# First feed-forward with four plain columns in place of six, and the third group's sums moved behind the last gate product

## The chip, the cores and the metric

The kernel runs on one core of a Trainium2 chip. The metric is device time in microseconds (us) of one execution; the time of a kernel is the median of several. Engines are named as in the profile: PE is TensorE's matrix product, PEld its weight loads, DVE is VectorE, ACT is ScalarE, POOL is GpSimd, SP issues most transfers.

## What is computed

The reference is a trunk of two layers on 512 positions of 1024 channels, in float32. Each layer has a half-step feed-forward, a mixer (a bidirectional state-space scan in layer 0, neighbourhood attention in layer 1), a second half-step feed-forward and a gated embedding:

```python
def swiglu(x, w_gu, w_down):
    g, u = jnp.split(x @ w_gu, 2, axis=-1)
    return (jax.nn.silu(g) * u) @ w_down

for i in range(DEPTH):
    h = h + 0.5 * swiglu(rmsnorm(h, ffn1_norm[i]), ffn1_w_gu[i], ffn1_w_down[i])
    h = h + mixer(rmsnorm(h, mix_norm[i]))
    h = h + 0.5 * swiglu(rmsnorm(h, ffn2_norm[i]), ffn2_w_gu[i], ffn2_w_down[i])
    gate = jax.nn.sigmoid(rmsnorm(h, ple_norm[i]) @ ple_w_gate[i])
    h = h + gate * rmsnorm(p[i] @ ple_w_proj[i], ple_post_norm[i])
```

So there are four feed-forwards. The inner width is 2816, which is 22 columns of 128.

## The kernel before

Everything is kept transposed: 128 channels on the partitions, the 512 positions along the free dimension, so `h` is eight tiles of 128 x 512. Full precision comes from splitting each operand in a high and a low part (ACT casts the high part, L231, L327; DVE subtracts it, L233, L328) and three matmuls for each product: high by high (L298), high by low (L301) and low by high (L302). A **weight unit** is 128 x 1024 numbers; three split units may be ready at a time (`bufs=3` of `wh` and `wl`), and `prep_next` splits the next one in the order that `plan` lists. `unit` takes one and refills.

A feed-forward (`ffn`) goes through its 22 columns in five chunks, `FIRST` for the first one of the kernel, `OTHERS` for the other three. `ffn_order` lists the steps:

- **Plain columns**: those of the first chunk, six in the first feed-forward, four in the others. `gate_up` forms the gate product and the other product of a column, two units of 24 matmuls each. They use `h` times the gain, without the norm; the reciprocal norm `R` is ready only after the first matmuls (`spread`, L379, then L381 to L388), and `activate` (L474 to L478) multiplies the products by it, applies the activation and splits the result into `mids[f]`.
- **Pairs of output tiles**: the down products of the first chunk for output tiles 0 to 3, two side by side (`side_by_side`). They need `mids` of all columns of the chunk.
- **Blocks**: the other columns two at a time. A pair of columns, both gate and other product, is a product of 2 x 2 blocks, done with seven block products in place of eight (`block`, matmuls at L539). Each block has one weight unit that is a sum or difference of the pair's quadrants (formed on DVE at L254, L257, L259, L276) and one input that is a sum or difference of halves of the normed `h`. These inputs, `xs`, are made once for each feed-forward by `sums(kk)` for four groups kk = 0 to 3 (L498 to L525), each with DVE work of about 5 us and casts on ACT; they need `R`. Blocks run in the order `TURN`: 0, 3, 1, 4, 5, 2, 6; blocks 0, 1, 2 and 6 take matmuls of 512 and 256 positions, the others three of 256. Every block reads all four groups.
- **Down products**, spread among the next chunk's blocks (L614, L629 add them to `h`).

In the first feed-forward columns 0 and 1 are computed while the inputs arrive (`first`), without `R`; column 2 is the first that ends with `R`.

Where `sums` is called before the change: in all feed-forwards group 0 stands behind the first `R` (L460, in `gate_up`). Each later plain column has one group in front of it (L604 and L605), and if one is left after the last plain column, it follows that column's activation (L469). In the first feed-forward this gives groups 0, 1, 2, 3 at columns 2, 3, 4, 5. In the others it gives groups 0, 1, 2 at columns 1, 2, 3 and group 3 behind column 3's activation.

The program order is not the engines' order. A planner (the tile framework's scheduler) walks over the program with costs of its own for each instruction and gives each engine's queue the ready instruction that comes first in the program, so a later instruction fills a gap in which an earlier one is not ready. The order is fixed when the kernel is built; on the chip each engine takes its instructions in that order. `tc.issue_after` adds an edge that keeps some of them behind another.

`plan` also sets when the first pair's four weight quadrants are fetched and summed: in the first feed-forward behind unit 6 (column 3), in the others behind unit 3.

Of the kernel before, what the change touches and what calls it, by code (L numbers as in the profile page):

```python
# [19 lines left out]
FF = 2816  # L20
NF = FF // P

FIRST = ((0, 6), (6, 10), (10, 14), (14, 18), (18, 22))
OTHERS = ((0, 4), (4, 8), (8, 12), (12, 16), (16, 22))
HT = T // 2
EPS = 1e-6
# [26 lines left out]
def ffn_order(chunks):  # L53

    for f in range(chunks[0][1]):
        yield "plain", f
    yield "pair", 0, 0
    yield "pair", 0, 2  # L60
    for c in range(1, len(chunks)):
        a, b = chunks[c]
        blocks = [(p, i) for p in range(a // 2, b // 2) for i in TURN]
        begun = d = 4 if c == 1 else 0
        for n, (p, i) in enumerate(blocks):
            yield "block", p, i
            while d < KD and (d - begun + 1) * len(blocks) <= (KD - begun) * (n + 1):
                yield "down", c - 1, d
                d += 1
    yield "between",  # L70
    for d in range(KD):
        yield "down", len(chunks) - 1, d
# [3 lines left out]
def trunk(ctx, tc, A, out):  # L76
# [76 lines left out]
    def plan():  # L153
# [3 lines left out]
        for i in range(stop):  # L157
            l, w = divmod(i, 4)
            if w in (0, 2):
                gu, gw, dn = [A[f"w_{x}{2 * l + w // 2}"] for x in ("gu", "gw", "dn")]  # L160
                chunks = FIRST if i == 0 else OTHERS
                plain = chunks[0][1]
# [115 lines left out]
    def unit(last=False):  # L278

        while (not last or not ready) and len(ready) < 3 and prep_next():  # L280
            pass
        return ready.pop(0)
# [10 lines left out]
    def gemm(pt, w, pairs, first=True, last=True, off=0, cols=slice(0, T), behind=False):  # L293
        hi, lo = w
        n = len(pairs)
        for k, xp in enumerate(pairs):
            sl = slice((off + k) * P, (off + k + 1) * P)
            m = te.matmul(out=pt, lhsT=hi[:, sl], rhs=part(xp, 0, cols), start=first and k == 0, stop=False)  # L298
            if behind and k == 0:
                tc.keep_in_program_order(m)  # L300
            te.matmul(out=pt, lhsT=hi[:, sl], rhs=part(xp, 1, cols), start=False, stop=False)  # L301
            gemm.last = te.matmul(out=pt, lhsT=lo[:, sl], rhs=part(xp, 0, cols), start=False,  # L302
                                  stop=last and k == n - 1)

    def side_by_side(pts, pairs, mid=None, at=4, then=None):

        ws = [unit() for _ in pts]
        k = len(pairs) - 1
        for pt, w in zip(pts, ws):
            c = min(at, k) if mid and pt is pts[-1] else k  # L310
            gemm(pt, w, pairs[:c], last=False)
            if mid and pt is pts[-1] and at <= k:
                mid()
            if then and c < k:
                gemm(pt, w, pairs[c:c + 1], first=False, last=False, off=c)
                then()
                c += 1
            if c < k:
                gemm(pt, w, pairs[c:k], first=False, last=False, off=c)
        for pt, w in zip(pts, ws):  # L320
            gemm(pt, w, pairs[k:], first=False, off=k)
        if mid and at > k:
            mid()
# [102 lines left out]
    def ffn(norm, nxt, between=None, first=None, at=4):  # L426
        R = [None]
# [4 lines left out]
        def mid():  # L432
            norm.begin()
            ahead(norm)

        def gate_up(f):
            pg = mm_bank()
            if not (first and R[0] is None and f == 2):
                pu = mm_bank()
            if first and f < 2:  # L440
                held.append((f, pg, pu))
                if f == 1:
                    first([p for x in held for p in x[1:]], norm.pairs)
                    mid()
                return
            if f == 0 and not first:
                side_by_side((pg, pu), norm.pairs, mid, at, lambda: norm.spread(AF.Silu))
                held.append((f, pg, pu))
                return
            if R[0] is None:  # L450

                w, c = unit(), 1
                gemm(pg, w, norm.pairs[:c], last=False)
                if first or at > len(norm.pairs) - 1:
                    norm.spread(AF.Silu)
                R[0] = norm.end()
                gemm(pg, w, norm.pairs[c:], first=False, off=c)
                while held:
                    activate(*held.pop(0))
                sums(left.pop(0))  # L460
                if first:
                    pu = px_bank()
            else:
                gemm(pg, unit(), norm.pairs)
            gemm(pu, unit(), norm.pairs)
            held.append((f, pg, pu))
            while held:
                activate(*held.pop(0))
            if left and f == chunks[0][1] - 1:  # L469
                sums(left.pop(0))  # L470

        def activate(f, pg, pu):
            gm = t2()
            v.tensor_mul(out=gm, in0=pg, in1=R[0])  # L474
            s.activation(out=gm, in_=gm, func=AF.Silu)
            um = t2()
            v.tensor_mul(out=um, in0=pu, in1=R[0])
            v.tensor_mul(out=um, in0=um, in1=gm)  # L478
            m = md(F32R)
            split(m, um, None)  # L480
            mids[f] = m
# [118 lines left out]
        made, left, owed = None, [0, 1, 2, 3], []  # L600
        chunks = FIRST if first else OTHERS
        for what, *a in ffn_order(chunks):
            if what == "plain":
                if left and R[0] is not None:  # L604
                    sums(left.pop(0))  # L605
                gate_up(a[0])
            elif what == "block":

                if between and a in ([chunks[-1][0] // 2, 0], [NF // 2 - 1, 4]):
                    next(between)  # L610
                block(*a)
                for d, pt in owed:
                    with tc.issue_after(block.last.ins):
                        v.scalar_tensor_tensor(out=h[d], in0=pt, scalar=0.5, in1=h[d], op0=ALU.mult, op1=ALU.add)  # L614
                owed = []
            elif what == "between":
                made = between and next(between)
            else:
                c, d = a
                last = c == len(chunks) - 1  # L620
                mine = [mids[f] for f in range(*chunks[c])]
                if what == "pair":
                    pts = [(mm_bank if d else px_bank)() for _ in range(2)]
                    side_by_side(pts, mine)
                    owed += [(d, pts[0]), (d + 1, pts[1])]
                    continue
                pt = mm_bank() if last else px_bank()
                gemm(pt, unit(last and d == KD - 1), mine)
                v.scalar_tensor_tensor(out=h[d], in0=pt, scalar=0.5, in1=h[d], op0=ALU.mult, op1=ALU.add)  # L629
                if last:  # L630
                    nxt(d)
                    if 1 < d < 5 and made is not None:
                        made[d - 1]()
# [905 lines left out]
    def first(pts, pairs):  # L1539
        done_ = [0] * 4  # L1540
        here, cut_ = 0, [0] * 4
        for o in order:
            if isinstance(o, int):
                here = o + 1
            else:
                cut_[o[0]] += 1
            for u in range(4):
                while done_[u] < min(here, 4 * cut_[u]):
                    k = done_[u]
                    gemm(pts[u], begun[u][2:], pairs[k:k + 1], first=k == 0, last=k == KD - 1, off=k)  # L1550
                    done_[u] += 1
        prep_next()

        with tc.issue_after(splits[-1].ins):
            for k in range(KD):
                n.count(k, True)
        while len(ready) < 3:
            prep_next()
# [17 lines left out]
def prepare(inp):  # L1576
    import numpy as np

    def units(w):
        k, n = w.shape[0] // P, w.shape[1] // P  # L1580
        return w.reshape(k, P, n, P).transpose(2, 1, 0, 3).reshape(n, P, k * P)
# [6 lines left out]
    for i in (1, 2):  # L1588
        gu = f[f"ffn{i}_w_gu"]
        for l in range(DEPTH):  # L1590
            k = 2 * l + i - 1
            plain = (OTHERS if k else FIRST)[0][1]
            g_ = units(gu[l]).reshape(2, NF, P, 1024).transpose(1, 0, 2, 3)
# [82 lines left out]
```

## Time and profile before

| what | value |
|---|---|
| median of 3 runs | 2274.69 us (2274.47 to 2274.8) |
| the profiled execution | 2274.88 us |
| its span, first to last instruction | 2273.0 us |
| granted TensorE clock | 0.999 |
| matmuls at L539 (blocks), four feed-forwards | 35 pairs, 4760 matmuls |

A page of the profile has busy time by engine, the chain of work that ended last, and groups of instructions. The timeline lists one engine's instructions: start in us, duration, engine, line, operation, tiles written and read, sizes, count; a bracket behind it gives idle time of the engine before it and what ended that. The chain of waits lists what the end of the execution hung on: start, length, engine and line. A row of the windows gives busy time of each engine in a stretch. Durations of matmuls are modelled, so their starts are what counts: a stream of 128 x 512 matmuls has durations of 0.39 us and starts 0.23 us apart. DVE's durations overlap by some 0.08 us with the next one's.

### The profile page before, as it was taken

To read this page: it belongs to the slowest core of one execution; us is meant where nothing else is said; L and a number is where in the kernel's file an instruction comes from. 1 tells how busy PE (TensorE), PEld (TensorE's weight loads), DVE (VectorE), ACT (ScalarE), POOL (GpSimd) and SP (SyncE) were. 2 spreads that over 40 slices of the span, in tenths; PEclk is the share of its full clock that TensorE was granted. 3 is DMA by queue.
4 is the path that set the end of the run, shared out by engine and by line. 5 is a ranking of instruction groups with operands and counts; after the bars stand their busy time and mean duration, and the time that the engine had idled before them with its cause. 6 is when DMAs were issued, how large, how long until landed. Compare 5 with 4: busy or idle time off the path is not lost.

```text
span 2273.0 us, 33245 instructions
## 1 busy us (share of the span) xinstructions
PE 2265.7 (100%) x12458; PEld 1948.5 (86%) x12458; DVE 1823.0 (80%) x2711; ACT 1284.3 (57%) x2335; POOL 327.9 (14%) x261
## 2 busy tenths in 40 slices
PE   9999999999999999999999999999999999999999
PEld 7888888888888888888888888888888888988887
DVE  8788878988888958988885898888668758888866
ACT  6444445777677765544457555444557655544563
POOL 0000001345555651000003100000110010000020
PEclk9999999999999999999999999999999999999999
DMA  5323324444444643322323332332557732333232
GB/s 198 114 77 107 107 78 140 162 154 140 146 141 143 208 146 120 116 98 85 102 89 115 108 102 88 98 107 78 173 176 228 227 117 92 103 107 107 79 102 75
DMA packets 105089, 281.56 MB, mean 124 GB/s; under 512 B 13008, under 2 KB 13904, under 8 KB 104928
## 3 DMA queue, kind: packets, MB, share of 16 engines
q1 hardware_dynamic: 104640, 279.30, 37.8%
q8 instruction: 98, 1.61, 0.3%
q14 instruction: 63, 0.52, 0.1%
q10 hardware_dynamic: 288, 0.14, 0.0%
HBM read 259.70 MB, written 13.40 MB: 120 GB/s over the span
## 4 chain that ended last, share of the span: by engine, by line
PE 96%; DVE 3%; ACT 1%; issue 0%; DMA 0%; POOL 0%; SPq 0%; DVEq 0%; POOLq 0%
PE ps L539 31%; PE ps L298 19%; PE ps L302 19%; PE ps L301 19%; PE ps L1023 1%; PE ps L982 1%; PE ps L1377 1%; PE ps L1003 1%; PE ps L1431 1%; PE ps L938 1%; PE ps L927 1%; PE ps L1420 1%; DVE wl L233 0%; DVE md L328 0%; PE ps L1411 0%
## 5 line engine op out<-in xcount | busy, mean ns | idle before, releaser
L298 PE MATMUL ps<-md,wh 128*128 128x512 f32 (+1 forms) x2032 | 796.0, 392 | 0.9 <-ACT md L327 0.9
L302 PE MATMUL ps<-md,wl 128*128 128x512 f32 (+1 forms) x2032 | 790.5, 389 | 0.2 <-DVE wl L233 0.2
L301 PE MATMUL ps<-md,wh 128*128 128x512 f32 (+1 forms) x2032 | 790.1, 389 | 0.0
L231 ACT CAST wh<-wr 128x1024 fp32r<-128x1024 f32 (+2 forms) x395 | 351.7, 892 | 417.4 <-PE ps L301 200.3
L233 DVE TENSOR_TENSOR wl<-wr,wh 128x1024 fp32r<-128x1024 f32 (+2 forms) x395 | 417.6, 1058 | 97.4 <-ACT wh L231 91.6
L302 PEld LDWEIGHTS ps<-md,wl 128*128 128x128 f32 x2032 | 381.5, 188 | 82.3 <-DVE wl L233 1.5
L298 PEld LDWEIGHTS ps<-md,wh 128*128 128x128 f32 x2032 | 381.6, 188 | 77.8 <-ACT md L327 1.4
L301 PEld LDWEIGHTS ps<-md,wh 128*128 128x128 f32 x2032 | 382.0, 188 | 74.0 <-DVE md L598 0.5
L539 PE MATMUL ps<-md,wh 128*128 128x256 f32 (+1 forms) x1610 | 367.2, 308 | 0.0
L539 PE MATMUL ps<-sc,wh 128*128 128x512 f32 (+1 forms) x1190 | 362.3, 357 | 0.0
L364 POOL TENSOR_TENSOR sq<-sq,sq 128x512 f32<-128x512 f32 x71 | 100.9, 1422 | 1612.1 <-ACT sq L360 1261.7
L233 DVE TENSOR_TENSOR wl<-md,wh 128x1024 fp32r<-128x1024 f32 x175 | 214.0, 1223 | 113.6 <-ACT wh L231 112.8
L231 ACT CAST wh<-md 128x1024 fp32r<-128x1024 f32 x175 | 183.8, 1051 | 200.9 <-PE ps L539 129.0
L539 PEld LDWEIGHTS ps<-md,wh 128*128 128x128 f32 x1610 | 263.7, 190 | 20.3
L539 PE MATMUL ps<-md,wl 128*128 128x256 f32 x980 | 276.4, 282 | 0.0
L539 PE MATMUL ps<-sc,wl 128*128 128x256 f32 x980 | 275.7, 281 | 0.0
L539 PEld LDWEIGHTS ps<-sc,wh 128*128 128x128 f32 x1190 | 210.0, 188 | 34.6
L539 PEld LDWEIGHTS ps<-sc,wl 128*128 128x128 f32 x980 | 185.2, 189 | 3.2
L539 PEld LDWEIGHTS ps<-md,wl 128*128 128x128 f32 x980 | 186.1, 190 | 0.0
L827 DVE SCALAR_TENSOR_TENSOR t<-ps,ccw,t 128x510 f32<-128x510 f32 (+1 forms) x180 | 133.3, 743 | 10.5 <-ACT t L820 7.9
L629 DVE SCALAR_TENSOR_TENSOR hs<-ps,hs 128x512 f32<-128x512 f32 x144 | 98.7, 685 | 49.9 <-PE ps L302 49.6
L565 DVE TENSOR_TENSOR t<-ps,t 128x256 f32<-128x256 f32 x280 | 113.4, 417 | 14.0 <-ACT t L562 12.8
(214 smaller groups left out, 2446.4 us busy)
## 6 DMA issues: line engine op xcount, KB each, us to landing
wr<-in_w_gw_dram SPq DMA_DIRECT2D x70, 512.0 KB, 3.3
md<-in_w_gw_dram SPq DMA_DIRECT2D x70, 512.0 KB, 4.5
wr<-in_w_in_dram SPq DMA_DIRECT2D x65, 512.0 KB, 3.2
wr<-in_w_dn_dram SPq DMA_DIRECT2D x128, 256.0 KB, 2.6
wr<-in_w_gu_dram SPq DMA_DIRECT2D x32, 512.0 KB, 3.2
hs<-crow SPq DMA_DIRECT2D x64, 256.0 KB, 3.7
wr<-in_w_dn_dram SPq DMA_DIRECT2D x32, 384.0 KB, 3.1
wr<-in_w_qkv_dram SPq DMA_DIRECT2D x24, 512.0 KB, 4.0
```

What stands on the lines that cost most here:

```text
L231: splits.append(s.copy(out=hi[:, :n], in_=raw[:, :n]))
L233: split_raw.low = v.tensor_sub(out=lo[:, :n], in0=raw[:, :n], in1=hi[:, :n])
L298: m = te.matmul(out=pt, lhsT=hi[:, sl], rhs=part(xp, 0, cols), start=first and k == 0, stop=False)
L301: te.matmul(out=pt, lhsT=hi[:, sl], rhs=part(xp, 1, cols), start=False, stop=False)
L302: gemm.last = te.matmul(out=pt, lhsT=lo[:, sl], rhs=part(xp, 0, cols), start=False, stop=last and k == n - 1)
L364: (v if fast else g).tensor_add(out=self.acc, in0=self.acc, in1=q)
L539: mm = lambda o, w, x, st, sp_: te.matmul(out=o, lhsT=w, rhs=x, start=opens and st, stop=sp_, skip_group_check=not opens)
L565: whole.last = v.tensor_add(out=o, in0=pt[j][:, :HT], in1=o)
L629: v.scalar_tensor_tensor(out=h[d], in0=pt, scalar=0.5, in1=h[d], op0=ALU.mult, op1=ALU.add)
L827: v.scalar_tensor_tensor(out=a[:, lo:hi], in0=src[:, lo + o:hi + o], scalar=w(j), in1=a[:, lo:hi], op0=ALU.mult, op1=ALU.add)
L927: te.transpose(out=pt[:, cs(i)], in_=src[:, cs(c)], identity=ident)
L938: te.matmul(out=pt[:, cs(c)], lhsT=bt[:, dr, cs(c)], rhs=ct_[:, dr, cs(c)], start=True, stop=True)
```

## The change

The first feed-forward gets the same chunks as the others: four plain columns, then nine pairs as blocks. Its columns 4 and 5, until now plain, become the first pair of blocks, the down products of the first chunk have four columns in place of six, and those of the last chunk six in place of four. The two other edits move `sums`: behind the last plain column's activation all groups that are left are summed, and in feed-forwards two to four no group is summed in front of the last plain column. So the groups stand at columns 1 and 2, and groups 2 and 3 behind column 3's activation; in the first feed-forward groups 0 and 1 at columns 2 and 3, and groups 2 and 3 behind column 3's activation.

```diff
-FIRST = ((0, 6), (6, 10), (10, 14), (14, 18), (18, 22))
+FIRST = ((0, 4), (4, 8), (8, 12), (12, 16), (16, 22))
 OTHERS = ((0, 4), (4, 8), (8, 12), (12, 16), (16, 22))
...
             held.append((f, pg, pu))
             while held:
                 activate(*held.pop(0))
-            if left and f == chunks[0][1] - 1:
+            while left and f == chunks[0][1] - 1:
                 sums(left.pop(0))
...
         chunks = FIRST if first else OTHERS
         for what, *a in ffn_order(chunks):
             if what == "plain":
-                if left and R[0] is not None:
+                if left and R[0] is not None and (first or a[0] < chunks[0][1] - 1):
                     sums(left.pop(0))
                 gate_up(a[0])
```

## The prediction

> **What bounds the kernel now.** I read the page first, then PE's timeline, the chain of waits and DVE's timeline around the place where a feed-forward goes over from plain columns to blocks. The page:
>
> ```profile
> span 2273.0 us, 33245 instructions
> ...
> PE 2265.7 (100%) x12458; PEld 1948.5 (86%) x12458; DVE 1823.0 (80%) x2711; ACT 1284.3 (57%) x2335; POOL 327.9 (14%) x261
> ...
> PE 96%; DVE 3%; ACT 1%; issue 0%; DMA 0%; POOL 0%; SPq 0%; DVEq 0%; POOLq 0%
> ```
>
> TensorE (PE) is never without work for long, and the chain that ended last is its own for 96%: a matmul saved is time saved, as long as VectorE (DVE) keeps up. DVE's 80% is a mean. The stages say more (a row has the stretch, its length, then the busy us of PE, of its weight loads, of DVE, ScalarE (ACT) and GpSimd, each with its instructions in brackets, then clock, DMA share and GB/s):
>
> ```profile
> 30.40:89.57 59.17, 59.17 (x263) 48.97 (x261) 46.79 (x85) 29.52 (x51) 0.00 (x0) 1.00 0.30 96
> 896.90:939.00 42.10, 42.10 (x186) 34.62 (x186) 42.05 (x78) 23.23 (x43) 0.00 (x0) 1.00 0.30 98
> 146.00:300.00 154.00, 154.00 (x919) 136.86 (x919) 124.78 (x175) 72.53 (x110) 0.00 (x0) 1.00 0.31 99
> ```
>
> The first row is the first feed-forward from the norm to its first block, six columns: DVE has 46.8 us of work in 59.2. The second is the second feed-forward, four columns: DVE is busy in 42.05 of 42.10 us. The third is blocks: 81%, so a backlog is worked off there. So DVE has some 12 us to spare ahead of the first feed-forward's blocks, and none ahead of the others'. The change takes the first one from the first kind to the second.
>
> **The columns that become blocks.** PE's timeline around those 59 us, and one pair's seven blocks in the chain of waits:
>
> ```profile
> 29.91 0.39 PE L379 MATMUL ps<-sq,mean 128*128 128x512 f32 x1
> ...
> 30.38 0.40 PE L298 MATMUL ps<-md,wh 128*128 128x512 f32 x1
> ...
> 89.57 0.39 PE L539 MATMUL ps<-sc,wh 128*128 128x512 f32 x1
> ```
> ```profile
> 89.73 8.51 PE ps L539 x56
> ...
> 98.47 2.86 PE ps L539 x24
> ...
> 105.22 5.71 PE ps L539 x40
> ...
> 112.07 2.78 PE ps L539 x16
> ```
>
> Between 30.38 and 89.57 the code has 21 matmuls left of the third column's gate product, 24 of its other product, 3 x 48 for three columns and 4 x 18 for four output tiles: 261, so 0.2268 us each. Two columns are 96 matmuls, 21.77 us. A pair as blocks is 136 matmuls, 56 + 24 + 40 + 16 in the rows: 8.51 + 2.86 + 5.71 + 2.78 = 19.86 us. The down products stay 22 matmul triples for each output tile, only cut at other places, so they cost the same. The trade saves 1.9 us of PE time.
>
> Against it speaks that blocks need 40 more weight loads per pair, and the page has a load at 190 ns:
>
> ```profile
> L539 PEld LDWEIGHTS ps<-md,wh 128*128 128x128 f32 x1610 | 263.7, 190 | 20.3
> ```
>
> But 40 block matmuls with 40 loads went by in 5.71 us, 143 ns each, less than one load alone. The loads overlap. [...]
>
> **DVE ahead of the first block.** This is the disputed cost. After R (the reciprocal norm) is there, DVE must make four gate products, split the weights of what PE does next, and sum four groups (`sums`) before block 0 can run. The second feed-forward does the same list now, and shows its price:
>
> ```profile
> 896.95 0.69 DVE L474 TENSOR_TENSOR t<-ps,rt 128x512 f32<-128x512 f32 x1
> ...
> 898.15 1.21 DVE L233 TENSOR_TENSOR wl<-wr,wh 128x1024 fp32r<-128x1024 f32 x1
> ...
> 903.83 0.68 DVE L478 TENSOR_TENSOR t<-t,t 128x512 f32<-128x512 f32 x1
> ...
> 918.59 1.21 DVE L233 TENSOR_TENSOR wl<-wr,wh 128x1024 fp32r<-128x1024 f32 x1
> ...
> 920.73 0.68 DVE L474 TENSOR_TENSOR t<-ps,rt 128x512 f32<-128x512 f32 x1
> ...
> 923.13 1.40 DVE L498 SCALAR_TENSOR_TENSOR t<-hs,cst,rt 128x512 f32<-128x512 f32 x2
> ...
> 929.28 0.68 DVE L474 TENSOR_TENSOR t<-ps,rt 128x512 f32<-128x512 f32 x1
> ...
> 934.62 0.68 DVE L328 TENSOR_TENSOR md<-t,md 128x512 fp32r<-128x512 f32 x1
> ...
> 936.56 0.68 DVE L233 TENSOR_TENSOR wl<-wr,wh 128x512 fp32r<-128x512 f32 x1
> ...
> 937.83 1.22 DVE L233 TENSOR_TENSOR wl<-wr,wh 128x1024 fp32r<-128x1024 f32 x1
> 938.97 1.22 DVE L233 TENSOR_TENSOR wl<-md,wh 128x1024 fp32r<-128x1024 f32 x1
> ```
> ```profile
> 939.70 0.39 PE L539 MATMUL ps<-sc,wh 128*128 128x512 f32 x1
> ```
>
> From the first product (896.95) to the end of block 0's split (938.97) are 42.0 us; PE begins block 0 at 939.70, so the cover there is only 0.7 us. The first feed-forward has less to do after its R, since more weights are ready by then:
>
> ```profile
> 29.68 1.22 DVE L259 TENSOR_TENSOR wr<-wr,wr 128x1024 f32<-128x1024 f32 x1
> ...
> 34.05 0.69 DVE L474 TENSOR_TENSOR t<-ps,rt 128x512 f32<-128x512 f32 x1
> ...
> 43.81 1.21 DVE L233 TENSOR_TENSOR wl<-wr,wh 128x1024 fp32r<-128x1024 f32 x1
> ```
>
> The three sums of weight quadrants (L254, L257, L259) are done by 30.8, and of the eight column splits only the one at 43.81 is left, where the second feed-forward has five, at 898.15 the first and at 918.59 the last. That is 3 + 4 = 7 instructions less. From 898.15 to 903.83 stand five of these kinds, 1.136 us each, so it is 8.0 us less: 34.05 + 42.0 - 8.0 = 68.1. PE, unhindered, is there after 141 matmuls (21 + 24 + 48 + 4 x 12) at 30.38 + 141 x 0.2268 = 62.4. Block 0's first matmul needs no low part, so it can start 0.2 before 68.1: PE waits 5.5 us. DVE keeps nothing in hand before 34.05, because all this needs R, and R comes as early as before.
>
> The ends. If the planner puts block 0's split ahead of the part of the last `sums` that only later blocks read (934.62 to 937.83 without the 0.7 us split at 936.56, 2.5 us), PE waits 3.0. If the fourth output tile's split, which stands at 936.56 inside the last `sums`, comes behind it, 13 matmuls (2.9 us) follow it after 67.0: block 0 at 69.9, a wait of 7.5. I take 5.5, the order of the second feed-forward. PE will wait once earlier: it ends column four at 62.4 - 48 x 0.2268 = 51.5, while DVE gets to that column's product at about 53.5 (43.81, a split of 1.1, and the 8.55 from 920.73 to 929.28) and needs some 3 to 4 us for it. That wait lies inside the 5.5. The transfers are no part of it: these waits come to
>
> ```profile
> ACT wh L231 <- DMA wr<-in_w_gu_dram: 9.2, 6, 3.5
> ```
>
> in all, under DVE's backlog, and the four output tiles' loads shrink from 384 to 256 KB.
>
> **The third group behind the last gate product.** In feed-forwards two to four this moves `sums(2)` (about 5 us of DVE) behind column three's activation; nothing is added or removed. It can only help where PE waited for that activation, which is the third feed-forward (PE and DVE):
>
> ```profile
> 1330.13 0.39 PE L301 MATMUL ps<-md,wh 128*128 128x512 f32 x1
> 1330.67 0.50 PE L302 MATMUL ps<-md,wl 128*128 128x512 f32 x1 [0.16 <-DVE wl L233]
> ...
> 1332.40 0.39 PE L298 MATMUL ps<-md,wh 128*128 128x512 f32 x1
> 1333.72 0.73 PE L298 MATMUL ps<-md,wh 128*128 128x512 f32 x2 [0.93 <-ACT md L327]
> ...
> 1340.97 0.28 PE L539 MATMUL ps<-sc,wl 128*128 128x256 f32 x1
> ```
> ```profile
> 1324.38 1.41 DVE L498 SCALAR_TENSOR_TENSOR t<-hs,cst,rt 128x512 f32<-128x512 f32 x2
> ...
> 1339.09 1.22 DVE L233 TENSOR_TENSOR wl<-wr,wh 128x1024 fp32r<-128x1024 f32 x1
> 1340.23 1.21 DVE L233 TENSOR_TENSOR wl<-md,wh 128x1024 fp32r<-128x1024 f32 x1
> ```
>
> Starts 0.54 and 1.32 us apart instead of 0.23: 1.4 us lost, with the two slow starts behind them about 1.5. `sums(2)` stands at 1324.38, in front of that activation, so the wait goes. What is late next is block 0's split, whose end (1340.23) hangs on DVE's unchanged total: of 1.5 us only 1340.97 - 1340.23 = 0.7 is kept. I take -0.7; the ends are 0 and -1.5. The second and fourth had no such wait: 0.
>
> **Sum** against the profiled 2274.88: -1.9 + 5.5 - 0.7 = +2.9, or 2277.8; the median is 0.2 below that execution, so **2277.6**. With the ends: -1.9 + 3.0 - 1.5 = -0.4 to -1.9 + 7.5 = +5.6, so 2274.3 to 2280.3. That is this case's own range. 0.2% is 4.5 us, about what a measurement of this kernel can tell from no change.
>
> **The rivals.**
>
> *DVE waits for PE with the sums queued behind it (slower).* DVE takes its instructions in the order that the planner wrote. With `sums(2)` behind the last activation in the program, DVE may reach L477 of column three (the second product) before PE has made it, and the sums that used to fill that time stand behind the wait. In the second feed-forward the product ends at 939.70 - 48 x 0.2274 = 928.8; without `sums(2)` DVE would be there at about 925.2 (923.13 + a low part, a split and L474, 0.68 each): 3.6 us idle, less the 0.7 of cover, 2.9 us; the same in the fourth, which I take as alike. In the third the product ends at 1340.97 - 1.5 - 10.9 = 1328.6 and DVE is there at 1326.4: 2.2 us more behind 1340.23, +1.5 in place of -0.7. Together 8.0 more: +10.9, 2285.6. It decides once DVE idles over 0.7 us there. For it: the cover is thin. Against it: the planner does not keep program order; it fills gaps, as between L474 at 896.95 and L478 of the same activation at 903.83, where it put five other instructions. [...] Chance 0.15, with anything up to that price.
>
> *The move does nothing.* The planner fills DVE with `sums(2)` as now, and the third feed-forward's waits stay: +3.6, 2278.3. For it: nothing else is ready on DVE at that time. Chance 0.10.
>
> *The cover holds.* If DVE could get the first feed-forward's list done by 62.4, PE would not wait: -1.9 - 0.7 = -2.6, 2272.1. Against it: 34 us of work in 28. Chance 0.06.
>
> *The loads bind.* 40 loads of 190 ns exposed are 7.6 us: +10.5, 2285.2. The 143 ns speak against it. Chance 0.02.
>
> **How the numbers follow.** My case has 0.64, of which 0.10 lies beyond +4.5 (the late order, or further small waits as blocks begin behind a backlog). Slower: 0.10, 0.15, 0.02 of the move that does nothing and 0.02 for the loads: 0.29. Faster: no case gives it; 0.03 for what I have not seen. Same: 0.68. The range of 2274.0 to 2282.5 leaves out the cover that holds, 0.03 of the unseen, half of the queue rival and the loads: about 0.19.
>
> **What would show it.** Right: nine pairs of L539 runs in the first feed-forward, its first about 68 us into the span instead of 89.7; DVE without idle time from 34 to 68; PE with about 5.5 us of waits between 51 and 68, for the fourth column's cast (L327) and for L233 or L525; the waits at 1330 gone; block 0 of the second and fourth as late after their norm as now. Wrong: PE's first block near 62 (cover), DVE idle ahead of L477 (queue), blocks over 20 us per pair (loads), or time moved in the stages between the feed-forwards, which I take as unchanged.

## The result and the profile after

| kernel | median | lowest to highest |
|---|---|---|
| before | 2274.8 us (5 runs) | 2274.47 to 2275.22 |
| after | 2298.08 us (5 runs) | 2297.5 to 2299.1 |

After takes 1.0103 times as long as before (95% interval 1.0092 to 1.0114): 23.3 us slower. The prediction was 2277.6 us, with no change that can be told as the likeliest outcome and 2282.5 as the upper end. It was wrong.

The page of the changed kernel, the lines that answer to those shown of before:

```profile
span 2296.2 us, 33340 instructions
PE 2274.3 (99%) x12498; PEld 1956.6 (85%) x12498; DVE 1831.7 (80%) x2726; ACT 1290.0 (56%) x2345; POOL 329.7 (14%) x261
PE 96%; DVE 3%; issue 0%; ACT 0%; DVEq 0%
```

PE's share goes from 100% to 99%, and its busy time is up by only 8.6 us on a span that is 23.2 us longer. To see where the time came in, I take one instruction that occurs once in each norm, the first matmul of `spread` (L379), as a milestone. The rows have count, durations in ns, then the first and last start. Before:

```profile
L379 PE MATMUL ps<-sq,mean x2: 394/394/394, 29.9 to 359.2; 128*128 128x512 f32 x2
L379 PE MATMUL ps<-sq,mean x2: 392/393/394, 841.3 to 892.8; 128*128 128x512 f32 x2
L379 PE MATMUL ps<-sq,mean x3: 394/394/395, 1223.0 to 1295.4; 128*128 128x512 f32 x3
L379 PE MATMUL ps<-sq,mean x1: 394/394/394, 1640.2 to 1640.2; 128*128 128x512 f32 x1
L379 PE MATMUL ps<-sq,mean x2: 394/395/396, 2207.1 to 2230.1; 128*128 128x512 f32 x2
```

After:

```profile
L379 PE MATMUL ps<-sq,mean x2: 394/394/394, 29.3 to 365.4; 128*128 128x512 f32 x2
L379 PE MATMUL ps<-sq,mean x2: 392/393/394, 847.3 to 898.8; 128*128 128x512 f32 x2
L379 PE MATMUL ps<-sq,mean x3: 394/394/397, 1234.6 to 1307.0; 128*128 128x512 f32 x3
L379 PE MATMUL ps<-sq,mean x1: 394/394/394, 1656.7 to 1656.7; 128*128 128x512 f32 x1
L379 PE MATMUL ps<-sq,mean x2: 394/396/397, 2230.3 to 2253.3; 128*128 128x512 f32 x2
```

Each milestone's delay against before: 29.3 - 29.9 = -0.6 as the first feed-forward goes over to its norm, 6.2 behind it, 6.0 ahead of the second, 11.6 behind it, 16.5 behind the third, 23.2 behind the fourth. So each feed-forward gives away its own share: 6.8, 5.6, 4.9 and 6.7 us. Between the feed-forwards the delay changes by 0.2 us at most. What PE and DVE wait for that they did not wait for before (us in total, times, longest):

```profile
PE ps L302 <- DVE wl L233: 13.5, 4, 4.4
PE ps L539 <- ACT wh L231: 2.7, 4, 1.1
```
```profile
DVE t L477 <- PE ps L302: 8.1, 3, 3.5
```

Four waits for the low part of a weight unit, one in each feed-forward, and DVE idle at L477 in three of them, which before never happened. The second feed-forward in the timelines of after, DVE first:

```profile
930.72 0.68 DVE L328 TENSOR_TENSOR md<-t,md 128x512 fp32r<-128x512 f32 x1
934.95 0.69 DVE L477 TENSOR_TENSOR t<-ps,rt 128x512 f32<-128x512 f32 x1 [3.55 <-PE ps L302]
936.76 1.41 DVE L498 SCALAR_TENSOR_TENSOR t<-hs,cst,rt 128x512 f32<-128x512 f32 x2
945.93 1.42 DVE L525 TENSOR_TENSOR md<-t,md 128x256 fp32r<-128x256 f32 x4
947.28 1.82 DVE L233 TENSOR_TENSOR wl<-wr,wh 128x512 fp32r<-128x512 f32 x2
```
```profile
944.49 0.51 PE L539 MATMUL ps<-sc,wh 128*128 128x256 f32 x2 [0.51 <-ACT wh L231]
948.01 0.50 PE L302 MATMUL ps<-md,wl 128*128 128x512 f32 x1 [3.02 <-DVE wl L233]
...
948.65 0.63 PE L301 MATMUL ps<-md,wh 128*128 128x512 f32 x1
949.08 0.63 PE L302 MATMUL ps<-md,wl 128*128 128x512 f32 x1
```

Read them together. DVE has been at L477 since 931.4 with 10 us of sums (L498 to L525) queued behind it, and idles 3.55 us until PE has the product. Then it does both groups in one piece. Only at 947.28, behind the last of them, comes the split that the last pair of output tiles needs (the row joins it with block 0's, which follows it), and PE, whose queue stands at that pair's L302, waits 3.02 us. And then something that the prediction has nowhere: the matmuls behind the wait start 0.43 us apart (948.65, 949.08), where the same shape goes at 0.23 otherwise. The windows of after show why (stretch, length; busy us of PE, its loads, DVE, ACT, POOL; the last but two is the granted clock):

```profile
66.60:70.90 4.30, 4.30 (x10) 3.44 (x11) 2.15 (x2) 0.07 (x1) 0.00 (x0) 0.50 0.68 222
71.30:75.00 3.70, 3.70 (x27) 3.42 (x27) 1.90 (x3) 2.27 (x4) 0.00 (x0) 1.00 0.00 1
...
948.50:951.80 3.30, 3.30 (x10) 2.52 (x9) 1.73 (x2) 0.00 (x0) 0.00 (x0) 0.50 0.79 245
1353.40:1357.70 4.30, 4.30 (x12) 3.43 (x11) 1.55 (x2) 0.68 (x1) 0.00 (x0) 0.50 0.74 243
1939.00:1942.50 3.50, 0.51 (x2) 0.30 (x2) 3.50 (x10) 1.83 (x5) 0.00 (x0) 0.89 0.00 0
1942.50:1948.50 6.00, 5.94 (x16) 4.78 (x17) 2.85 (x4) 1.04 (x1) 0.00 (x0) 0.50 0.56 178
```

Behind each of the four waits TensorE runs at half its clock, 0.50 in rows of 3.3 to 6.0 us. The clock need not wait for PE to resume: in the row of 1939.00, where PE waits until 1942.56, its mean is already 0.89. PE's busy time hides this, since a slow matmul counts as busy: in the row of 948.50 PE is busy for 3.30 of 3.30 us, with ten matmuls. The mean granted clock of the page fell only from 0.999 to 0.995.

The first feed-forward shows the same, with a longer wait (PE, then DVE):

```profile
59.74 0.73 PE L539 MATMUL ps<-sc,wh 128*128 128x512 f32 x2
61.61 0.50 PE L539 MATMUL ps<-sc,wh 128*128 128x256 f32 x2 [1.13 <-ACT wh L231]
66.53 0.80 PE L302 MATMUL ps<-md,wl 128*128 128x512 f32 x1 [4.42 <-DVE wl L233]
...
70.54 0.63 PE L302 MATMUL ps<-md,wl 128*128 128x512 f32 x1
70.97 0.42 PE L539 MATMUL ps<-sc,wl 128*128 128x256 f32 x1
```
```profile
65.79 1.82 DVE L233 TENSOR_TENSOR wl<-wr,wh 128x512 fp32r<-128x512 f32 x2
```

The waits here are 1.13 + 4.42 = 5.55 us; behind them stand ten matmuls at half clock, and block 0's low products begin at 70.97. Ahead of the last pair's tail PE's queue has two high products of block 0 (59.74) and two of block 3 (61.61), whose 128 x 256 inputs mark them; the 1.13 us are the wait for the high part of block 3's weights.

### The profile page after: what moved, and what is told of

Its sections match the earlier page's. It is cut to its first block, busy times and chain, and to the rows that moved or that the text cites. A ratio compares the mean times of both kernels' runs of the same rounds, so it can differ in the third digit from the quotient of the medians.

```text
span 2296.2 us, 33340 instructions
## 1 busy us (share of the span) xinstructions
PE 2274.3 (99%) x12498; PEld 1956.6 (85%) x12498; DVE 1831.7 (80%) x2726; ACT 1290.0 (56%) x2345; POOL 329.7 (14%) x261
## 4 chain that ended last, share of the span: by engine, by line
PE 96%; DVE 3%; issue 0%; ACT 0%; DVEq 0%
PE ps L539 31%; PE ps L302 19%; PE ps L298 19%; PE ps L301 19%; PE ps L1023 1%; PE ps L982 1%; PE ps L1377 1%; PE ps L1003 1%; PE ps L1431 1%; PE ps L938 1%; PE ps L927 1%; PE ps L1420 1%; DVE t L498 1%; DVE md L328 0%; DVE sc L525 0%; PE ps L1411 0%
## 5 line engine op out<-in xcount | busy, mean ns | idle before, releaser
L302 PE MATMUL ps<-md,wl 128*128 128x512 f32 (+1 forms) x2000 | 782.3, 391 | 13.5 <-DVE wl L233 13.5
L298 PE MATMUL ps<-md,wh 128*128 128x512 f32 (+1 forms) x2000 | 786.5, 394 | 0.0
L301 PE MATMUL ps<-md,wh 128*128 128x512 f32 (+1 forms) x2000 | 780.3, 390 | 0.0
L302 PEld LDWEIGHTS ps<-md,wl 128*128 128x128 f32 x2000 | 377.5, 189 | 95.6 <-DVE wl L233 15.4
L539 PE MATMUL ps<-md,wh 128*128 128x256 f32 (+1 forms) x1656 | 377.8, 308 | 0.0
L539 PE MATMUL ps<-sc,wh 128*128 128x512 f32 (+1 forms) x1224 | 373.5, 358 | 2.7 <-ACT wh L231 2.7
L233 DVE TENSOR_TENSOR wl<-md,wh 128x1024 fp32r<-128x1024 f32 x180 | 220.2, 1224 | 110.9 <-ACT wh L231 110.0
L231 ACT CAST wh<-md 128x1024 fp32r<-128x1024 f32 x180 | 189.1, 1051 | 207.9 <-PE ps L539 121.6
L539 PE MATMUL ps<-md,wl 128*128 128x256 f32 x1008 | 284.5, 282 | 0.0
L539 PE MATMUL ps<-sc,wl 128*128 128x256 f32 x1008 | 284.2, 282 | 0.0
L539 PEld LDWEIGHTS ps<-sc,wh 128*128 128x128 f32 x1224 | 216.4, 189 | 40.2 <-ACT wh L231 4.9
L539 PEld LDWEIGHTS ps<-sc,wl 128*128 128x128 f32 x1008 | 191.4, 190 | 3.8
```

The source lines that it names most:

```text
L231: splits.append(s.copy(out=hi[:, :n], in_=raw[:, :n]))
L233: split_raw.low = v.tensor_sub(out=lo[:, :n], in0=raw[:, :n], in1=hi[:, :n])
L539: mm = lambda o, w, x, st, sp_: te.matmul(out=o, lhsT=w, rhs=x, start=opens and st, stop=sp_, skip_group_check=not opens)
```

## The experiments

Two theories. **A**: each of the change's two parts (the new chunks, the moved sums) has its own price. In the first feed-forward DVE has a longer list ahead of block 0; in the other three it idles at L477. In all four the two late splits (last output tile, block 0) stand behind all the sums, so that DVE's delay reaches PE undiminished, and the wait then costs a second time through the clock. **B**, the rivals to it: the sums' place is harmless and only the amount of DVE work counts; or the slow clock is a mere sign of the wait and costs nothing of its own; or the first feed-forward's blocks cause what is seen in the later ones. Each run is given beside runs of the kernel before on the same chip (2274.6 to 2274.8 us).

**One part alone.** e1 has the new `FIRST` and the `while`, without the condition, so feed-forwards two to four are as before:

```diff
-                if left and R[0] is not None and (first or a[0] < chunks[0][1] - 1):
+                if left and R[0] is not None:
```

> Only the first feed-forward is changed (four plain columns, groups 2 and 3 behind column 3); feed-forwards two to four keep their order of before. Theory (the loss is made of separate DVE waits in each feed-forward, and the first one's share is 8.4 us of PE waits and slow clock less 1.9 us of saved matmuls): +6.5, 2281.3 us, first block at about 70 us as in the changed kernel. Rival (the loss is one effect, of the first feed-forward's late start on everything behind it): near 2298. Rival (the move of the third group alone costs): near 2274.

Measured: 2281.41 us, ratio 1.003 (1.0019 to 1.0042), +6.8. e2 has the condition and the `while`, with the first feed-forward as before:

```diff
-FIRST = ((0, 4), (4, 8), (8, 12), (12, 16), (16, 22))
+FIRST = ((0, 6), (6, 10), (10, 14), (14, 18), (18, 22))
```

> Only the third group is moved behind the last gate product in feed-forwards two to four; the first keeps six plain columns. Theory (DVE stands at L477 of column 3 with both groups queued behind it, about 3.8 us in each of the three, and the late start costs more behind it): +17, 2291.5 us, DVE idle ahead of L477 for about 3.5 us three times. Rival (these waits come only from the first feed-forward's late start): near 2275.

Measured: 2291.68 us, 1.0073 (1.0058 to 1.0088), +17.1. The parts add up to 23.9 where both together cost 23.3, and the milestones agree: feed-forwards two to four lose 5.6, 4.7 and 6.7 us in e2's trace, 5.6, 4.9 and 6.7 in that of after. So the parts act independently as far as these runs can tell, and three quarters of the loss is the move that I had priced at a gain of 0.7. In e2's waits the same row stands as in after, now three times:

```profile
PE ps L302 <- DVE wl L233: 9.1, 3, 3.0
```

**The place of group 2.** e3 is e2 with group 2 put back by one step only: still behind column 3's products in the program, but ahead of its activation, and so ahead of L477.

```diff
+            if len(left) > 1 and f == chunks[0][1] - 1:
+                sums(left.pop(0))
             while held:
                 activate(*held.pop(0))
```

> As the move alone (six plain columns first), but in feed-forwards two to four the third group stands in the program behind column 3's products and ahead of its activation, so its weight units are prepared in the order of the changed kernel while DVE may fill the time before L477 with the group. Theory (it is the place of the group in DVE's queue): the waits go, 2274.8 us within 2. Rival (it is the weight units that are prepared in another order, or the group's later reading of h): stays near 2291.

Measured: 2274.77 us, 1.0001 (0.9991 to 1.0011): all 17.1 us are gone. The work is the same, and group 3 still follows the activation; what counts is whether `sums(2)` stands ahead of or behind L477 in DVE's queue. In e3's second feed-forward the group begins ahead of it and DVE doesn't idle there (two lines were added ahead, so L500 is what was L498, L479 what was L477):

```profile
922.95 0.74 DVE L500 SCALAR_TENSOR_TENSOR t<-hs,cst,rt 128x512 f32<-128x512 f32 x1
...
930.38 0.68 DVE L479 TENSOR_TENSOR t<-ps,rt 128x512 f32<-128x512 f32 x1
```

**The order behind it.** In the first feed-forward, e4 puts the fourth group behind the first pair of output tiles, so that the splits of both pairs and of block 0 can come ahead of it:

```diff
-            while left and f == chunks[0][1] - 1:
+            while left and f == chunks[0][1] - 1 and not (first and len(left) == 1):
                 sums(left.pop(0))
...
+                    if left:
+                        sums(left.pop(0))
```

> As the first part alone, but in the first feed-forward the fourth group stands in the program behind the first pair of output tiles, so that the last output tile's split and block 0's split come ahead of its tail in DVE's queue. Theory (DVE's total sets block 0, the late split adds 2 us and the long wait a slow clock): the wait shrinks from 6.5 to between 3 and 5.5 us; 2276 to 2278.5. Rival (the wait is the order alone): no wait, 2273. Rival (the order is nothing, all of it is DVE's total): 2281.

Measured: 2277.23 us, 1.0012 (1.0002 to 1.0021), +2.6 in place of e1's +6.8. No wait is over 2.12 us now, and the clock stays whole (1.000 over the run). e4's DVE and PE:

```profile
60.25 0.68 DVE L233 TENSOR_TENSOR wl<-wr,wh 128x512 fp32r<-128x512 f32 x1
61.86 1.21 DVE L233 TENSOR_TENSOR wl<-wr,wh 128x1024 fp32r<-128x1024 f32 x1
...
67.27 1.21 DVE L233 TENSOR_TENSOR wl<-md,wh 128x1024 fp32r<-128x1024 f32 x1
```
```profile
63.39 0.28 PE L539 MATMUL ps<-sc,wl 128*128 128x256 f32 x1
...
68.53 0.39 PE L539 MATMUL ps<-sc,wl 128*128 128x256 f32 x1 [2.12 <-DVE wl L233]
```

The output tile's split stands at 60.25, not at 65.79, block 0's at 61.86, and block 0's low products begin at 63.39, not at 70.97. Behind the fourth group is now the split of the block after it (67.27), and that is what PE still waits for, 2.12 us at 68.53. e9 lets the fourth group wait for both pairs (`if left and d:`).

> As the kernel with the split ahead (four plain columns first), with the fourth group behind both pairs of output tiles in the first feed-forward, so that block 3's split is ahead of it too. Theory (DVE's total of 34 us after the norm sets block 0 and block 3, whatever the order): the waits change place but stay 3 to 5 us, 2276.5 to 2278.5. Rival (a better order is all that is missing): waits under 2 us, 2274 or less.

Measured: 2277.25 us, 1.0012 (1.0002 to 1.0021), the same +2.5. This still later place gives no more, so what is left doesn't seem to hang on this order.

e8 does in feed-forwards two to four what e4 does in the first, on top of e2:

```diff
-            while left and f == chunks[0][1] - 1:
+            while left and f == chunks[0][1] - 1 and (first or len(left) > 1):
                 sums(left.pop(0))
...
+                    if left:
+                        sums(left.pop(0))
```

> The move alone (six plain columns first), with the fourth group in feed-forwards two to four traced behind the first pair of output tiles, so the last output tile's split and block 0's split come ahead of its tail; DVE still stands at L477 with both groups behind it. Theory (DVE's idle time ahead of L477 is 3.8 us, 0.7 of it covered, and late split and slow clock make the rest): DVE idle there stays near 3.6 us, PE waits fall to about 3 us in each and come in shorter pieces, clock 1.0: 2281 to 2283.5. Rival (the wait at L477 alone makes it all): 2290. Rival (the late split makes it all): 2275.

Measured: 2277.95 us, 1.0014 (1.0005 to 1.0024), +3.2 where e2 has +17.1. I had expected more to remain. The idle time at L477 is as long as ever (the row of L477: 8.4 us in three), yet the two splits now stand ahead of the fourth group, the last L498 below, and behind the third group alone (e8's second feed-forward, which begins some 6 us earlier than in after):

```profile
  PE ps L302: 8.4, 3
```
```profile
928.56 0.69 DVE L477 TENSOR_TENSOR t<-ps,rt 128x512 f32<-128x512 f32 x1 [3.55 <-PE ps L302]
...
934.91 0.69 DVE L233 TENSOR_TENSOR wl<-wr,wh 128x512 fp32r<-128x512 f32 x1
936.52 1.22 DVE L233 TENSOR_TENSOR wl<-wr,wh 128x1024 fp32r<-128x1024 f32 x1
937.66 1.41 DVE L498 SCALAR_TENSOR_TENSOR t<-hs,cst,rt 128x512 f32<-128x512 f32 x2
```

So with the same idle time a feed-forward loses 5.7 us on average in one order (17.1 / 3) and 1.1 in the other (3.2 / 3). By the milestones these 3.2 lie in the second and the fourth (1.7 and 1.6 us), where DVE idles 3.55 us; the third loses nothing.

e12 does the same to the kernel before (the call behind the last activation removed, the call behind the pair added), where DVE is not late.

> The kernel before (six plain columns, third group ahead of the last plain column), with the fourth group traced behind the first pair of output tiles in feed-forwards two to four. Theory (where DVE is not late, the place of the splits is worth nothing; the 1.7 us of waits in the third feed-forward come from the third group and stay): 2274.7 within 0.7. Rival (the earlier splits help by themselves): 2273 or less.

Measured: 2274.73 us, 1.0 (0.9991 to 1.0008). Where DVE is not late, the order is worth nothing that can be measured; it decides what a late DVE costs.

**The clock by itself.** e5 is e2 with 13 matmuls whose result is overwritten, put on PE ahead of the last pair of output tiles, so that PE is busy while it waits:

```diff
+                    if d and not first:
+                        for _ in range(13):
+                            tc.keep_in_program_order(te.matmul(out=pts[1], lhsT=mean[1.0], rhs=part(mine[0], 0, slice(0, T)),
+                                                               start=True, stop=True))
```

> The move alone, with 13 idle matmuls (2.9 us) ahead of the last pair of output tiles in feed-forwards two to four, into a bank that the real product then starts anew; the result is the same. DVE's queue is the one of the move alone. Theory (the long PE wait of 3.2 us in each makes the clock fall to 0.5 for 3.4 to 6.8 us, which costs some 7 us over the three): with the wait filled PE idles about 1 us, the clock stays at 1.0, 2284.5 us within 1.5. Rival (the slow matmuls behind the wait have another cause): the clock rows stay, and 2291 or, if the idle matmuls do not fit in the wait, up to 2300.

Measured: 2285.83 us, 1.0048 (1.0033 to 1.0063), +11.0. DVE's queue is as in e2, with the same 3.55 us idle at L477 in the second feed-forward; the idle matmuls take 13 x 0.227 = 2.95 us, as long as the wait of 3.02 us that they fill, so what differs is the clock. e2 and then e5, second feed-forward:

```profile
937.00:942.00 5.00, 1.47 (x7) 0.80 (x6) 5.00 (x13) 2.89 (x6) 0.00 (x0) 1.00 0.00 0
942.00:945.30 3.30, 3.30 (x9) 2.55 (x9) 1.95 (x2) 0.00 (x0) 0.00 (x0) 0.50 0.72 211
```
```profile
939.00:945.00 6.00, 5.24 (x25) 4.08 (x24) 5.36 (x10) 2.32 (x5) 0.00 (x0) 1.00 0.26 93
```

So 2291.68 - 2285.83 = 5.9 us of e2's 17.1 are the slow clock, about 2 us for each wait. e10 does the same to e1, with 18 matmuls in the first feed-forward.

> The first part alone (four plain columns first), with 18 idle matmuls (4.1 us) ahead of the last pair of output tiles in the first feed-forward, into a bank that the real product then starts anew; the result is the same. Theory (of the 8.8 us lost there some 2.5 are the clock at 0.5 for 6.8 us): 2279 within 1, clock rows without 0.5. Rival (the clock costs nothing): 2281.4 or more.

Measured: 2278.73 us, 1.0019 (1.0009 to 1.0028), clock 1.000: 2.7 of e1's 6.8 us are the clock. The idle matmuls changed the planner's order a little here (PE now waits 0.95 us for a cast before them), so this figure is rougher than e5's: by the milestones of the first feed-forward it is 2.2.

**Both mended.** e11 is the whole change with the fourth group behind the first pair in all four feed-forwards.

```diff
-            while left and f == chunks[0][1] - 1:
+            while len(left) > 1 and f == chunks[0][1] - 1:
                 sums(left.pop(0))
...
+                    if left:
+                        sums(left.pop(0))
```

> The whole change, with one more edit: in all four feed-forwards the fourth group is traced behind the first pair of output tiles. Theory (the first part costs 2.6 us and the move 3.2 us once the splits stand ahead of the fourth group, and the parts add): 2280.5 us within 1.5, clock 1.0, DVE still idle ahead of L477 for 8 us in all. Rival (the parts hang together, the first feed-forward's late blocks upset the later ones): 2285 or more.

Measured: 2280.36 us, 1.0026 (1.0017 to 1.0035), +5.7, which is e4 and e8 added (2.6 + 3.2). 17.7 of the 23.3 us are won back, and it is still slower than before.

**Less work on DVE.** If DVE's total sets what is left of the first feed-forward, taking work off it should turn the loss into a gain. e6 is e4 with the four subtractions of each `sums` (L501, L502, L520, L521) on POOL, e7 the kernel before with the same:

```diff
-            v.tensor_sub(out=a[:, lo_], in0=x[0][:, hi_], in1=x[0][:, lo_])
+            g.tensor_sub(out=a[:, lo_], in0=x[0][:, hi_], in1=x[0][:, lo_])
...
```

> Four plain columns first with the split ahead (as the kernel with the fourth group behind the first pair), and in all feed-forwards the four half-width subtractions of each group (5.4 us of DVE per feed-forward) on POOL, which is idle there. Theory (DVE's total is what holds block 0): the waits in the first feed-forward fall from 4.1 to under 1.5 and the 1.7 of the third go: 2271.5 to 2273.5. Rival (POOL at about 0.75 us each and the way there and back set the pace instead, or DVE slows beside POOL): 2275 to 2280.

> The kernel before (six plain columns) with the same four subtractions of each group on POOL. Theory: only the 1.7 us of waits in the third feed-forward go, 2273; it stands above the four-column kernel with POOL by up to 1.9 us. Rival (POOL's latency or its effect on DVE costs): 2275 or more.

Measured: 2304.36 us, 1.0133 (1.0116 to 1.015) for e6 and 2300.64 us, 1.0114 (1.0098 to 1.0129) for e7. Both expected gains missed by over 25 us; of the rivals, e7's (2275 or more) came true and e6's (up to 2280) fell short. First the same subtraction where DVE does it, in the timeline of after; then the group of e6's page, and a subtraction of e6's DVE beside them:

```profile
1343.40 0.42 DVE L501 TENSOR_TENSOR t<-t 128x256 f32<-128x256 f32 x1
```

```profile
L501 POOL TENSOR_TENSOR t<-t 128x256 f32<-128x256 f32 x16 | 30.1, 1882 | 159.1 <-DVE t L498 159.1
```
```profile
51.66 1.22 DVE L328 TENSOR_TENSOR md<-t,md 128x512 fp32r<-128x512 f32 x1
```

1.88 us for what takes DVE 0.42, while DVE's own 128x512 subtraction at L328 goes from 0.68 (930.72 in after) to 1.22. L328 has a mean of 879 ns in e7, where 681 is the mean of before (42 instructions in each). Beside e6's row at 51.66 POOL has L520 at 51.41 for 0.92 us and L521 at 52.41 for 1.07. No run here shows what slows DVE there. The groups come later instead of sooner, and the casts on ACT and the splits queued behind them with them. So these two runs don't test whether DVE's total is what is left: they changed DVE's speed as well as its work. How their 26 to 30 us divide was not followed further; the slow clock is in them too (a mean of 0.997 in e6 and 0.996 in e7).

## Why the prediction was wrong

**The trade of columns for blocks** (-1.9). No run isolates it, since DVE's longer list comes with it; what the runs give is the two together, +2.6 in the best order tried (e4). e4's trace shows 0.5 of the 1.9: from the first norm to the next PE is busy for 328.31 us (30.20 to 361.20), before for 328.80 (30.40 to 359.20). Part of a late start counts as busy (before, at 1330.67: 0.54 us behind the matmul ahead of it in place of 0.23, with 0.16 counted as idle), so the rest may be there and be eaten by such starts; that is not shown.

**The first feed-forward's wait** (5.5, with ends at 3.0 and 7.5). The mechanism was right, and so was DVE's list: from its first L474 (33.46 in after) to the end of block 0's split (65.79 + 1.82) are 34.2 us, where 34.05 were foreseen. That the wait measured 5.55 us is luck, though, for the order was the one of the upper end, priced at 7.5: the last output tile's split stands behind the whole of `sums`, and PE has to finish that tile before block 0's low products. It came to less than 7.5 since ten matmuls stood there and not 13, and PE took four products of blocks 0 and 3 ahead of them. The earlier wait, for column four's cast, which was to be a part of the 5.5, did not occur. And the price of the wait was incomplete: e10 shows 2.7 us more for the clock. Of the +6.8 the order explains 1.5 beside that (e10 to e4: 2278.73 - 2277.23; by the milestones 2.6, so clock and order are told apart only within about 1 us), and 2.6 are what DVE's list costs in the best order, less what the trade saves; my early end had put that at -1.9 + 3.0 = +1.1.

**The third group behind the last gate product** (-0.7 for the third feed-forward, 0 for the others; e2 measured +17.1). This step failed. It reads "It can only help where PE waited for that activation", and rests on the sentence in the rivals that "it fills gaps". The planner did fill gaps elsewhere, but not this one: in its queue both groups stand behind L477. Presumably DVE was not early there by the planner's costs, which no run shows; on the chip it was. The queue rival, which I gave 0.15, came true in its mechanism, and nearly to the digit in its idle time: 3.6 us foreseen in the second feed-forward, 3.55 measured, and 3.55 again in the fourth (DVE in after, third and fourth feed-forward):

```profile
1337.99 0.69 DVE L233 TENSOR_TENSOR wl<-wr,wh 128x512 fp32r<-128x512 f32 x1 [0.52 <-ACT wh L231]
1339.66 0.69 DVE L477 TENSOR_TENSOR t<-ps,rt 128x512 f32<-128x512 f32 x1 [0.98 <-PE ps L302]
...
1929.50 0.69 DVE L477 TENSOR_TENSOR t<-ps,rt 128x512 f32<-128x512 f32 x1 [3.55 <-PE ps L302]
```

The third had 0.98 us there and 0.52 ahead of a split, against 2.2 foreseen. Its wait at 1330 did go, as predicted, but PE then waits 0.51 and 3.02 us at its last pair, as in the other two.

**The rival's price.** It too was far short: 2.9 us in the second and the fourth and 1.5 in the third, 7.3 for the move against e2's 17.1. Two terms were missing. First, I took the idle time less the cover of 0.7 us as the cost, as if the last thing DVE did were block 0's split in its old place. With both groups in one piece behind L477, the splits of the last output tile and of block 0 fell behind all of it, and PE's queue had ten matmuls waiting for the first of the two. I knew this order, as the upper end in the first feed-forward, and didn't carry it over to the others. Second, the clock.

**The clock** stands nowhere in the prediction. It is the step from a wait's length to its cost: I counted one microsecond for each. Put together, e2's 17.1 us are 5.9 for the clock (e2 to e5), 7.9 for the two splits' place (e5 to e8) and 3.2 that the idle DVE still costs in the best order (e8). These are differences of medians of different kernels, whose 95% intervals reach 0.1 to 0.15% (2 to 3 us) to either side, so the parts are rough. The division also follows the order in which the edits were taken: e8's order alone also rids PE of the long waits, and so of the slow clock. With 2.7 + 1.5 + 2.6 in the first feed-forward that is the 23.9 of the two parts, against 23.3.

Theory A holds. Of the rivals, that only DVE's amount of work counts falls with e3 and e8 (the same work, 16.9 and 13.7 us less than e2); that the clock is only a sign falls with e5 and e10; that the first feed-forward's blocks cause what is seen in the later ones falls with e1 and e2.

Open: why the planner left DVE idle at L477, as its costs are on no record; and whether the 2.6 us of the first feed-forward can go with less DVE work, since the only attempt at that slowed DVE down.

## What to carry to other kernels

Before moving work behind an instruction of an in-order queue, work out from the trace when that queue will get there and when its operand is ready; if it is early, it idles there (3.55 us here, with the sums queued behind), and whatever the other engine needs next should stand ahead of the moved work. TensorE, busy for 99% of the span, paid for waits of 0.51 + 3.02 and 1.13 + 4.42 us a second time, some 2 to 3 us each lost to half clock (e5, e10), so look at the granted clock of the microseconds behind a wait. With a wait cut to 2.12 us (e4) or filled with idle matmuls (e5, e10) that part was saved.

## What the runs showed of the hardware

**Half a clock behind a wait.** The granted clock fell to 0.50 with waits of 0.51 + 3.02 us and of 1.13 + 4.42 us, each pair parted by two short matmuls, in the fourth feed-forward before PE had resumed (a mean of 0.89 from 1939.00 to 1942.50, with PE waiting until 1942.56), and was still 0.50 through the windows shown, 3.3 to 6.0 us long, though PE was busy. Behind e4's single wait of 2.12 us it didn't fall: 1.00 from 68.00 to 72.00. What length of wait is enough isn't shown: e6 and e7 have a mean clock of 0.997 and 0.996, where before has 0.999, and no wait of PE that their profiles list is over 1.9 us.

**Fewer instructions on DVE, more time.** 64 short subtractions moved from DVE to POOL made a kernel whose POOL is busy for 14% of the span 26 us slower (e7), with a mean of 1.88 us for the first of each group on POOL against 0.42 on DVE, and DVE's own L328 at a mean of 879 ns in place of 681.
